# The second pass over the tokens in two pieces of 512, its operands kept by chunks of 128 tokens

## The chip, the cores and the metric

The kernel runs on one core of one Trainium2 chip. The metric is device time in microseconds (us): the median of three runs, 1899.62 us, lowest 1899.07, highest 1901.29. The profiled execution took 1902.07 us, of which 1900.3 us lie between its first and its last instruction (the span).

## The reference, cut to what matters

The program is one layer of a hybrid encoder over 2048 prompt tokens and 64 sample tokens of width 1024. A normed copy `h` of the input goes through one wide projection. Its columns feed two branches, a chunked state-space scan with a short convolution in front (SSD) and a bank of diagonal recurrences (S5). Both branches are gated and go through an output projection.

```python
h = rmsnorm(x, norm_g)
z_a, xbc, dt_raw, u_b, z_b = jnp.split(h @ w_in, IN_SPLITS, axis=-1)   # 1024 | 2048 | 16 | 1024 | 1024 columns
# SSD: xbc -> causal conv of 4 taps -> silu -> x, B, C; scan over blocks of tokens; * silu(z_a); grouped norm
# S5: u_b -> per-group diagonal recurrence -> gelu -> GLU; * silu(z_b)
out = jnp.concatenate([y_a, y_b], axis=-1) @ w_out
y = rmsnorm(x + out, final_norm_g)
```

Only `h @ w_in` is touched by the change, and of it the part for the last 1024 prompt tokens.

## The kernel before

**Two passes over the tokens.** The first pass (`st` = 0) takes the 64 sample tokens and the first 1024 prompt tokens, the second pass (`st` = 1) the other 1024. `phase_x` (L268) norms rows of 128 tokens, transposes them on TensorE into PSUM (`psx`) and splits every value into a rounded part and its rest: ScalarE writes the high part (L324), VectorE the low part (L326). The tokens of a pass are held in three pieces (L37): 320, 384 and 384 tokens in the first pass, 256, 384 and 384 in the second. Each piece has a high tile `hh` and a low tile `hl` of 8 rows of depth (`k`) by its tokens. The second pass writes into the same three pairs of tiles, so a piece of the second pass may be written once the piece of the first pass in that place has been read for the last time.

**The projection.** Weights come in blocks of 256 columns, in two halves of depth: `wblock` (L215) loads a half, ScalarE rounds it (`CAST whi`, L212) and VectorE forms the rest (`wlo`). Three halves can be held at a time, so a half is rounded only when the half three before it is no longer read. `proj_cm` (L232) takes 128 of these columns as the stationary operand and one piece of tokens as the moving one. It issues 24 matmuls for a piece (8 depths, three products each: high by high, high by low, low by high) into one of four PSUM banks. A run of 128 columns over all tokens of the second pass is thus 3 pieces, 72 matmuls. There are 32 such runs in the second pass: 16 in `phase_uz_block` (L345, the columns of the S5 input and gate, tile `psu`) and 16 in `conv_block` (L690, the columns that go through the convolution, tile `psr`). The gate of the SSD branch and dt (`proj_tm`, L242, tile `psz`) use chunks of 128 tokens as the stationary operand; there the piece only says where a chunk lies.

**What is woven between the pieces.** A piece ends in a `yield`. `weave` (L1286) runs one generator as the main line and after each of its yields advances side generators by a rate: the S5 recurrence `s5_steps` (L663) at rate 1 per yield, and the chunk scan `phase_s_chunks` (L840) at 1.8 to 2. A step of the S5 recurrence makes products on TensorE (`psi` in `s5_a`, `psy` in `s5_c`), several passes of ScalarE and VectorE, and scans on VectorE. A chunk of the SSD scan is a chain over three engines. `a1` puts transposes and one product into PSUM (`pA`) and scans decay products into `E` on VectorE; `a2` multiplies `E` by what is in `pA`; `b1` makes `pY` from `E` and from the state `h2`, and `pH`; `b2` adds `pH` to the state. So chunk c+1's product with the state waits until `b2` of chunk c is through.

**What sets the order.** The Tile scheduler takes the program in this written order and sets each engine's queue from it with its own estimates; an engine then runs its queue strictly in order, a waiting instruction holding what is behind it. Loads are issued by SyncE (SP), also in order.

Of the kernel before, what the change touches and what calls it, by code (L numbers as in the profile page):

```python
# [19 lines left out]
NS = 64  # L20
# [13 lines left out]
C_ZA, C_X, C_B, C_C, C_DT, C_U, C_ZB = 0, 1024, 2048, 2560, 3072, 3088, 4112  # L34


PIECES = ((320, 384, 384), (256, 384, 384))  # L37


ORDERED = {mybir.EngineType.Activation, mybir.EngineType.DVE}  # L40
# [3 lines left out]
def tile_hybrid_stream(  # L44
# [162 lines left out]
    hp = right.enter_context(tc.tile_pool(name="hp", bufs=1, side="right", reuse_waits="tile"))  # L207
    rawp = right.enter_context(tc.tile_pool(name="rawp", bufs=2, side="right", reuse_waits="tile"))
    wp = right.enter_context(tc.tile_pool(name="wp", bufs=3, side="right", reuse_waits="tile"))

    def split(hi, lo, raw):
        act.copy(out=hi, in_=raw)  # L212
# [18 lines left out]

    def proj_cm(ps, W, m0, piece):  # L232

        hi, lo, _ = piece
        for k in range(8):
            wh = W[0][k // 4][:, k % 4, m0:m0 + 128]
            wl = W[1][k // 4][:, k % 4, m0:m0 + 128]
            mm(ps, wh, hi[:, k], k == 0, False)
            mm(ps, wh, lo[:, k], False, False)
            mm(ps, wl, hi[:, k], False, k == 7)  # L240

    def proj_tm(ps, W, n, piece, off, nt):  # L242

        hi, lo, _ = piece
        for k in range(8):
            wh = W[0][k // 4][:, k % 4, 0:n]
            wl = W[1][k // 4][:, k % 4, 0:n]
            mm(ps, hi[:, k, off:off + nt], wh, k == 0, False)
            mm(ps, lo[:, k, off:off + nt], wh, False, False)
            mm(ps, hi[:, k, off:off + nt], wl, False, k == 7)  # L250

    def proj_smp(ps, W, n, piece):

        hi, lo, s2 = piece
        for k in range(8):
            wh = W[0][k // 4][:, k % 4, 0:n]
            wl = W[1][k // 4][:, k % 4, 0:n]

            def both():
                mm(ps[:, :n], s2[:, k], wh, k == 0, k == 7)  # L260
            if k < 7:
                both()
            mm(ps[:NS, :n], s2[:, k, 0:NS], wl, False, False)
            if k == 7:
                both()


    def phase_x(st, pcs, xpool):  # L268

        rows = [(xs, 0, NS)] if st == 0 else []  # L270
        rows += [(xp, 1024 * st + 128 * i, 128) for i in range(8)]
        g_bc = []
        live = {}

        def load(i):

            if i >= len(rows):
                return
            src, r0, n = rows[i]
            xt = xpool.tile([128, D], F32, tag="xt", name="xt", bufs=4)  # L280
            sp.dma_start(out=xt[:n], in_=src[r0:r0 + n, :])
            if not g_bc:
                g_bc.append(xpool.tile([128, D], F32, tag="g_bc", name="g_bc", bufs=1))
                sp.dma_start(out=g_bc[0], in_=norm_g[0:1, :].to_broadcast([128, D]))
            rs = cons.tile([128, 1], F32, tag="rs", name="rs", bufs=4)
            sq = xpool.tile([128, D], F32, tag="xsq", name="xsq", bufs=1)
            actf(sq[:n, :D], xt[:n], AF.Square, scale=1.0 / 32, accum_out=rs[:n])
            pool.tensor_scalar(out=rs[:n], in0=rs[:n], scalar1=1.0, scalar2=EPS, op0=ALU.mult, op1=ALU.add)
            pool.tensor_tensor(out=rs[:n], in0=rs[:n], in1=mhalf[:n], op=ALU.pow)
            live[i] = xt, rs  # L290

        def norm(i):
            if i >= len(rows):
                return
            n = rows[i][2]
            xt, rs = live[i]
            stt(xt[:n], xt[:n], rs[:n], g_bc[0][:n], ALU.mult, ALU.mult)

        load(0)
        load(1)  # L300
        norm(0)
        yield
        col = i = base = 0
        for j, (src, r0, n) in enumerate(rows):
            xn = live.pop(j)[0]
            if col == base + (PIECES[st][i] if pcs else 0):
                if pcs:
                    base += PIECES[st][i]
                    i += 1
                w = PIECES[st][i]  # L310
                hi = hp.tile([128, 8, PIECES[0][i]], F32R, tag=f"hh{i}", name=f"hh{i}")
                lo = hp.tile([128, 8, PIECES[0][i]], F32R, tag=f"hl{i}", name=f"hl{i}")
                s2 = None
                if st == 0 and i == 0:
                    s2 = hp.tile([128, 8, 2 * NS], F32R, tag="hs", name="hs")
                pcs.append((hi[:, :, :w], lo[:, :, :w], s2))
            off = col - base
            for q in range(2):
                ps = pj.tile([128, 4, 128], F32, tag="pj", name="psx")
                for k in range(4):  # L320
                    kk = 4 * q + k
                    nc.tensor.transpose(ps[:, k, :n], xn[:n, kk * 128:(kk + 1) * 128], ident[:n, :n])
                hv = pcs[i][0][:, 4 * q:4 * q + 4, off:off + n]
                act.copy(out=hv, in_=ps[:, :, :n])  # L324
                lv = pcs[i][1][:, 4 * q:4 * q + 4, off:off + n]
                tt(lv, ps[:, :, :n], hv.bitcast(F32), ALU.subtract)  # L326
                if n == NS:
                    pool.tensor_copy(out=s2[:, 4 * q:4 * q + 4, 0:NS], in_=hv.bitcast(F32))
                    pool.tensor_copy(out=s2[:, 4 * q:4 * q + 4, NS:], in_=lv.bitcast(F32))
            col += n  # L330
            norm(j + 1)
            load(j + 2)
            yield


    def kcols(st):

        if st == 0:
            return [(0, 0, 64, 0), (0, 64, 256, 9), (1, 0, 384, 41), (2, 0, 384, 89)], 137, 0
        return [(0, 0, 256, 0), (1, 0, 384, 32), (2, 0, 384, 80)], 129, 137  # L340

    def phase_uz_block(st, pcs, blk, kind):
        runs, K, c0 = kcols(st)
        W = wblock([((C_U if kind == "u" else C_ZB) + 256 * blk, 256)])
        piece_outer = st == 0 and blk == 3 and kind == "z"  # L345
        ubs, ths = {}, {}
        order = [(m, i) for i in range(3) for m in range(2)] if piece_outer else [(m, i) for m in range(2) for i in range(3)]
        for m, i in order:
            b = 2 * blk + m
            if i == 0:  # L350
                ubs[m] = big.tile([128, 8, 137], F32, tag="big", name="ub")
                pool.memset(ubs[m][:, :, 8:9] if st == 0 else ubs[m][:, :, 128:129], 0.0)
            ub = ubs[m]
            ps = pj.tile([128, 512], F32, tag="pj", name="psu")
            proj_cm(ps[:, :PIECES[st][i]], W, 128 * m, pcs[i])
            for (pi, off, n, k0) in runs:
                if pi != i:
                    continue
                nk = n // 8
                src = ps[:, off:off + n].rearrange("p (k s) -> p s k", s=8)  # L360
                dst = ub[:, :, k0:k0 + nk]
                if kind == "u":
                    act.copy(out=dst, in_=src)
                else:
                    actf(dst, src, AF.Silu)
            if i < 2:
                yield
                continue
            if kind == "u":
                for j in range(8):  # L370
                    pool.dma_start(out=U[8 * b + j, :, :, c0:c0 + K].rearrange("s c k -> c s k"),
                                   in_=ub[16 * j:16 * j + 16, :, :K])
            else:
                pool.dma_start(out=Z[:, 128 * b:128 * b + 128, c0:c0 + K].rearrange("s c k -> c s k"), in_=ub[:, :, :K])
            yield


    def prep_params(p, P):
# [311 lines left out]
    def conv_block(st, pcs, W, m0, blk, p):  # L690
# [6 lines left out]
        else:  # L697
            act.copy(out=R[:, 0:3], in_=carry[:, blk, :])
        o = 3
        for i in range(3):  # L700
            n = PIECES[st][i]
            ps = pj.tile([128, 512], F32, tag="pj", name="psr")
            proj_cm(ps[:, :n], W, m0, pcs[i])
            if st == 0 and i == 0:
# [3 lines left out]
            else:  # L708
                act.copy(out=R[:, o:o + n], in_=ps[:, :n])
                o += n  # L710
            yield
        if st == 0:
            act.copy(out=cnew[:, 0, :, blk], in_=R[:, 64:67])
            act.copy(out=carry[:, blk, :], in_=R[:, 1091:1094])
# [9 lines left out]
    def chunks(st):  # L724

        r = []
# [3 lines left out]
            for c in range(6):  # L730
                r.append((128, 1 + c // 3, 128 * (c % 3), 323 + 128 * c, 320 + 128 * c))
        else:
            r += [(128, 0, 0, 0, 1088), (128, 0, 128, 128, 1216)]
            for c in range(6):
                r.append((128, 1 + c // 3, 128 * (c % 3), 256 + 128 * c, 1344 + 128 * c))
        return r

    def phase_s_init(st, p):
# [547 lines left out]
    def weave(main, *sides):  # L1286

        acc = [0.0] * len(sides)
        for _ in main:
            for i, (g_, r_) in enumerate(sides):  # L1290
                acc[i] += r_
                while acc[i] >= 1.0:
                    acc[i] -= 1.0
                    next(g_, None)
# [5 lines left out]
    def take(g_, n):  # L1300

        for _ in range(n):
            next(g_, None)
            yield

    V = {}
    pcs = []
# [69 lines left out]
    weave(S[2], (S5, R5))  # L1377
    C = chks(2)
    weave(phase_uz_block(1, pcs, 3, "z"), (C, RB), (S5, R5))
    weave(take(S[3], 12), (C, 1), (S5, R5))  # L1380
    drain(C, S5)
    s5_out(p5, fin)
    aux.close()
# [67 lines left out]
```

## Time and profile before

| What | us |
|---|---|
| median of three runs | 1899.62 |
| profiled execution, span | 1902.07, 1900.3 |
| TensorE matmuls busy | 1831.1 (96%) |
| TensorE weight loads busy (beside the matmuls) | 1709.4 (90%) |
| VectorE, ScalarE, GpSimd busy | 1096.5 (58%), 908.6 (48%), 378.3 (20%) |
| span up to the first matmul of the second pass's pieces | 692.86 |
| from there to the last matmul of its convolutions | 572.24 |

TensorE is busy for all but 4% of the span. Its single matmuls overlap (the next one starts while the last one drains), so the duration that a row gives for one matmul is longer than the time that it costs; the cost is read from the distance between starts.

### The profile page before, as it was taken

What the parts mean: (1) busy time and instruction counts of PE and PEld (TensorE: products, weight loads), DVE (VectorE), ACT (ScalarE), POOL (GpSimd) and SP (SyncE); (2) the same over time, 40 slices, a digit from 0 to 9 for tenths busy, and PEclk for the clock granted to TensorE, in tenths of its full rate; (3) what the DMA queues carried; (4) which work ended last, traced back from release to release, by engine and by line L of the source; (5) the groups of instructions that cost most, each with busy time, mean ns of one, the idle gap of its engine ahead of it and who ended that gap; (6) DMA issues with size and microseconds to landing.
All of it is one profiled execution on the core that took longest, in us unless ns stands there. A gap on an engine that the chain in (4) does not pass through costs nothing. (4 is left out here: it accounts for less than half of the span.)

```text
span 1900.3 us, 31061 instructions
## 1 busy us (share of the span) xinstructions
PE 1831.1 (96%) x11400; PEld 1709.4 (90%) x11400; DVE 1096.5 (58%) x2157; ACT 908.6 (48%) x2505; POOL 378.3 (20%) x730
## 2 busy tenths in 40 slices
PE   7998999999899899999999999999999999999998
PEld 6998999999899799889989999998999988887886
DVE  5688687685767653776678567857544432212221
ACT  5466465545646633666666556656544421111110
POOL 3022314233332411032013301212211000001000
PEclk9999999999999999999999999999999999999999
DMA  5224545454444454456545754536455553313220
GB/s 165 76 72 101 155 105 137 127 137 103 121 128 111 143 137 119 139 153 182 152 136 164 206 159 125 152 95 178 134 161 161 186 181 92 97 56 95 92 86 34
DMA packets 197816, 244.69 MB, mean 129 GB/s; under 512 B 41696, under 2 KB 158432, under 8 KB 197664
## 3 DMA queue, kind: packets, MB, share of 16 engines
q1 hardware_dynamic: 170944, 167.49, 31.7%
q0 software_dynamic: 25136, 74.66, 13.4%
q8 instruction: 90, 1.47, 0.3%
q10 hardware_dynamic: 1584, 0.56, 0.2%
q14 instruction: 62, 0.51, 0.1%
HBM read 171.09 MB, written 75.75 MB: 130 GB/s over the span
## 5 line engine op out<-in xcount | busy, mean ns | idle before, releaser
L69 PE MATMUL psp<-whi,yy 128*128 128x512 f32 x1056 | 333.6, 394 | 1.3 <-ACT yy L212 1.3
L69 PE MATMUL psu<-hh,whi 128*128 128x384 f32 (+2 forms) x768 | 259.1, 337 | 0.8 <-DVE hl L60 0.8
L69 PE MATMUL psr<-hh,whi 128*128 128x384 f32 (+2 forms) x768 | 256.8, 335 | 3.1 <-ACT whi L212 3.1
L69 PE MATMUL psr<-hh,wlo 128*128 128x384 f32 (+2 forms) x768 | 249.4, 325 | 1.8 <-DVE wlo L60 1.8
L69 PE MATMUL psu<-hl,whi 128*128 128x384 f32 (+2 forms) x768 | 250.3, 326 | 0.0
L69 PE MATMUL psu<-hh,wlo 128*128 128x384 f32 (+2 forms) x768 | 250.1, 326 | 0.0
L69 PE MATMUL psr<-hl,whi 128*128 128x384 f32 (+2 forms) x768 | 249.9, 325 | 0.0
L69 PEld LDWEIGHTS psp<-whi,yy 128*128 128x128 f32 x1056 | 198.2, 188 | 48.9 <-ACT yy L212 1.5
L69 PE MATMUL psp<-wlo,yy 128*128 128x512 f32 (+1 forms) x544 | 214.8, 395 | 0.0
L69 PE MATMUL psz<-whi,hh 128*128 128x256 f32 (+1 forms) x512 | 151.4, 296 | 0.4 <-DVE dtr L60 0.4
L69 PEld LDWEIGHTS psr<-hh,whi 128*128 128x128 f32 x768 | 146.1, 190 | 4.5 <-ACT whi L212 3.3
L69 PE MATMUL psz<-whi,hl 128*128 128x256 f32 (+1 forms) x512 | 147.0, 287 | 1.4 <-DVE hl L60 1.4
L69 PEld LDWEIGHTS psr<-hh,wlo 128*128 128x128 f32 x768 | 145.7, 190 | 2.5 <-DVE wlo L60 2.3
L69 PEld LDWEIGHTS psu<-hh,whi 128*128 128x128 f32 x768 | 145.4, 189 | 2.1 <-DVE hl L60 1.0
L69 PEld LDWEIGHTS psr<-hl,whi 128*128 128x128 f32 x768 | 146.0, 190 | 1.2
L69 PE MATMUL psz<-wlo,hh 128*128 128x256 f32 (+1 forms) x512 | 147.0, 287 | 0.0
L69 PE MATMUL psg<-gh,glo 128*128 128x266 f32 x512 | 146.1, 288 | 0.9 <-DVE glo L60 0.9
L69 PE MATMUL psg<-gl,ghi 128*128 128x266 f32 x512 | 146.6, 289 | 0.0
L69 PEld LDWEIGHTS psu<-hl,whi 128*128 128x128 f32 x768 | 145.5, 189 | 1.1
L69 PEld LDWEIGHTS psu<-hh,wlo 128*128 128x128 f32 x768 | 145.3, 189 | 0.3
L69 PE MATMUL psg<-gh,ghi 128*128 128x266 f32 x512 | 144.0, 288 | 0.0
L60 DVE TENSOR_TENSOR wlo<-raw,whi 128x1024 fp32r<-128x1024 f32 (+1 forms) x80 | 97.9, 1225 | 78.9 <-ACT whi L212 77.3
(559 smaller groups left out, 3914.6 us busy)
## 6 DMA issues: line engine op xcount, KB each, us to landing
raw<-in_w_in_dram SPq DMA_DIRECT2D x64, 512.0 KB
tab<-TAB SPq DMA_DIRECT2D x64, 266.0 KB
xt<-in_x_prompt_dram SPq DMA_DIRECT2D x32, 512.0 KB
abc<-atd SPq DMA_DIRECT2D x64, 256.0 KB
TAB<-k POOLq DMA_DIRECT2D x32, 266.0 KB, 3.7
ut<-U SPq DMA_DIRECT2D x32, 266.0 KB
Y<-bs POOLq DMA_DIRECT2D x32, 266.0 KB, 3.8
G<-Y SPq DMA_DIRECT2D x128, 66.5 KB
```

The source lines that it names most:

```text
L60: dve.tensor_tensor(out=out, in0=a, in1=b, op=op)
L69: nc.tensor.matmul(out, lhsT=lhsT, rhs=rhs, start=start, stop=stop)
```

## The change

In the second pass there are two pieces of 512 tokens in place of 256, 384 and 384. One tile `HL` takes the place of the three pairs `hh` and `hl`. In the first pass its parts are laid out as the pairs were: each piece high then low, depth by tokens. In the second pass the same tile is laid out by chunks of 128 tokens: for each chunk, high and low, 8 depths of 128 tokens. The moving operand of a matmul of the second pass, 512 tokens of one depth, is then four runs of 128 elements that lie 2048 elements apart; the output in PSUM is one run of 512. A class `Piece` hides the two layouts. A yield of the second pass's pieces counts 1.5 in `weave`, so that the side work per run of 128 columns keeps its amount, and `take(S[3], 12)` becomes 8 because four runs now have 8 pieces.

```diff
-PIECES = ((320, 384, 384), (256, 384, 384))
+PIECES = ((320, 384, 384), (512, 512))
+PARTW = (1, 1.5)
+class Piece:
...
+    def mov(self, h, k):
+        if self.chunks is None:
+            return self.hl[h][:, k]
+        return self.chunks[:, :, h, k]
...
+    def put(self, h, q, off, n):
+
+        if self.chunks is None:
+            return self.hl[h][:, 4 * q:4 * q + 4, off:off + n]
+        return self.chunks[:, off // 128, h, 4 * q:4 * q + 4, :n]
...
+    HL = [hp.tile([128, 16 * sum(PIECES[0])], F32R, name="HL")]
+    HOFF = [16 * sum(PIECES[0][:i]) for i in range(3)]
...
-            mm(ps, wh, hi[:, k], k == 0, False)
-            mm(ps, wh, lo[:, k], False, False)
-            mm(ps, wl, hi[:, k], False, k == 7)
+            mm(ps, wh, piece.mov(0, k), k == 0, False)
+            mm(ps, wh, piece.mov(1, k), False, False)
+            mm(ps, wl, piece.mov(0, k), False, k == 7)
...
+                    pcs.append(Piece(w, chunks=HL[0][:, 8192 * i:8192 * i + 8192].rearrange("p (c h k t) -> p c h k t", c=4, h=2, k=8)))
...
-        return [(0, 0, 256, 0), (1, 0, 384, 32), (2, 0, 384, 80)], 129, 137
+        return [(0, 0, 512, 0), (1, 0, 512, 64)], 129, 137
...
-            if i < 2:
-                yield
+            if i < np_ - 1:
+                yield PARTW[st]
...
-        for _ in main:
+        for w in main:
             for i, (g_, r_) in enumerate(sides):
-                acc[i] += r_
+                acc[i] += r_ * (w or 1)
...
-    weave(take(S[3], 12), (C, 1), (S5, R5))
+    weave(take(S[3], 8), (C, 1), (S5, R5))
```

**ScalarE's queue, second pass, second weight block of the first convolutions.** Before: `bs<-b` and `bs<-psy` belong to the S5 recurrence, `cv` and `R` to the convolution, `whi` to the weights that TensorE needs next.

```order
L66 ACTIVATE cv<-cv 128x1024
L709 COPY R<-psr 128x384
L642 COPY bs<-b 64x532
L660 COPY bs<-psy 128x266
L643 ACTIVATE bs<-b 64x532
L660 COPY bs<-psy 128x266
L212 CAST whi<-raw 128x4x256
```

The same place now:

```order
L92 ACTIVATE cv<-cv 128x1024
L653 COPY b<-psi 128x265
L654 COPY bs<-psi 64x265
L655 ACTIVATE bs<-psi 64x265
L653 COPY b<-psi 128x265
L654 COPY bs<-psi 64x265
L655 ACTIVATE bs<-psi 64x265
L240 CAST whi<-raw 128x4x256
```

The rounding of the weights no longer stands behind `bs<-b`, which waits for VectorE's scans; the copies ahead of it wait only for the products `psi`.

**TensorE's queue, second pass, a chunk of the SSD scan amid the columns of the S5 input.** Before, a chunk's group of products is followed by S5 products and by matmuls of a piece:

```order
L69 MATMUL pY<-xd,E 128x64 x4
L69 MATMUL pY<-h_103,cv 128x256
L69 MATMUL pH<-xw,bt 128x256
L856 MATMUL pA<-ident,cv 128x128
L857 MATMUL pA<-ident,cv 128x128
L858 MATMUL pA<-ident,cv 128x128
L69 MATMUL pA<-cv 128x128
L69 MATMUL psy<-ut,ct 128x266
```

Now, at the fourth and fifth chunk of the first block that is woven:

```order
L95 MATMUL pY<-xd,E 128x64 x4
L95 MATMUL pY<-h_103,cv 128x256
L95 MATMUL pH<-xw,bt 128x256
L884 MATMUL pA<-ident,cv 128x128
L885 MATMUL pA<-ident,cv 128x128
L886 MATMUL pA<-ident,cv 128x128
L95 MATMUL pA<-cv 128x128
L95 MATMUL pY<-xd,E 128x64 x4
L95 MATMUL pY<-h_103,cv 128x256
L95 MATMUL pH<-xw,bt 128x256
```

Two chunks' groups stand one behind the other, with no matmul of a piece between the first chunk's `pH` and the second chunk's product with the state. This occurs three times in the second pass now and did not before.

**TensorE's queue, second pass, where that first woven block begins.** Before; `pA<-cv` (the product of the convolved B and C) stands a whole piece of 384 further on:

```order
L69 MATMUL psu<-hl_7463,whi 128x256
L856 MATMUL pA<-ident,cv 128x128
L857 MATMUL pA<-ident,cv 128x128
L858 MATMUL pA<-ident,cv 128x128
L69 MATMUL psi<-ut,bl 128x265 x2
L69 MATMUL psu<-hh_7657,whi 128x384
```

The same place now:

```order
L95 MATMUL psu<-HL,whi 128x512 x2
L884 MATMUL pA<-ident,cv 128x128
L885 MATMUL pA<-ident,cv 128x128
L886 MATMUL pA<-ident,cv 128x128
L95 MATMUL psi<-ut,bl 128x265
L95 MATMUL pA<-cv 128x128
L95 MATMUL psi<-ut,bl 128x265
L95 MATMUL psu<-HL,whi 128x512 x2
```

`pA<-cv` has moved up, from behind the second piece to behind the first.

## Rows read from the trace of the kernel before

**Rows 1.** The page: span, and TensorE's busy time (share of the span).

```profile
span 1900.3 us, 31061 instructions
PE 1831.1 (96%) x11400; PEld 1709.4 (90%) x11400; DVE 1096.5 (58%) x2157; ACT 908.6 (48%) x2505; POOL 378.3 (20%) x730
```

**Rows 2.** Windows: stretch, length, busy time (count) by engine, TensorE's granted clock, DMA.

```profile
692.86:1265.10 572.24, 557.03 (x3495) 533.28 (x3494) 394.59 (x667) 336.96 (x920) 109.14 (x223) 0.99 0.53 148
...
769.00:776.00 7.00, 5.78 (x20) 5.06 (x21) 5.68 (x7) 4.95 (x13) 0.00 (x0) 0.51 0.88 253
974.00:977.40 3.40, 3.40 (x14) 3.06 (x13) 1.44 (x3) 2.17 (x10) 0.00 (x0) 0.52 0.64 160
```

**Rows 3.** Timeline, TensorE, second pass: start, duration, line, tiles, shape.

```profile
692.86 0.28 PE L69 MATMUL psu<-hh,whi 128*128 128x256 f32 x1
...
695.70 0.34 PE L69 MATMUL psu<-hh,whi 128*128 128x384 f32 x1
...
704.09 0.28 PE L69 MATMUL psu<-hh,whi 128*128 128x256 f32 x1
...
737.77 0.27 PE L813 MATMUL pa<-ident,slots 128*128 128x128 f32 x1
```

**Rows 4.** Timeline, TensorE, output projection: the first matmul of a tile, and what follows it.

```profile
1582.90 0.48 PE L69 MATMUL psp<-wlo,yy 128*128 128x512 f32 x1
...
1605.18 0.38 PE L1146 MATMUL pso<-ident,ya 128*128 128x128 f32 x2
```

**Rows 5.** Groups of ScalarE over the whole span: count, busy us and mean ns.

```profile
L324 ACT CAST hh<-psx 128x512 fp32r<-128x512 f32 x32 | 17.4, 589 | 2.3 <-PE psx L322 1.9
L212 ACT CAST yy<-pso 128x512 fp32r<-128x512 f32 x32 | 17.2, 590 | 56.1 <-PE pso L1146 56.1
```

**Rows 6.** Timeline, TensorE, second pass, a piece that follows S5 products, and the next.

```profile
922.44 0.47 PE L69 MATMUL psr<-hh,whi 128*128 128x256 f32 x1
...
925.47 0.34 PE L69 MATMUL psr<-hh,whi 128*128 128x384 f32 x1
```

**Rows 7.** Timeline of ScalarE, then what TensorE's `psr` waited for (us, times).

```profile
763.38 0.46 ACT L709 COPY R<-psr 128x384 f32<-128x384 f32 x1
765.92 0.63 ACT L642 COPY bs<-b 64x532 f32<-64x532 f32 x1 [2.08 <-DVE b L640]
...
767.89 1.05 ACT L212 CAST whi<-raw 128x1024 fp32r<-128x1024 f32 x1
...
  ACT whi L212: 3.1, 1
  DVE wlo L60: 1.2, 1
```

**Rows 8.** Groups of TensorE in 967.3 to 977.4 and in 1161 to 1170.

```profile
L69 PE MATMUL pA<-cv 128*128 128x128 f32 x4 | 1.1, 372 | 2.2 <-ACT cv L66 2.2
...
L69 PE MATMUL pA<-cv 128*128 128x128 f32 x4 | 0.9, 300 | 1.3 <-ACT cv L66 1.3
```

**Rows 9.** Groups of the convolution, whole span: ScalarE, VectorE, ScalarE.

```profile
L66 ACT ACTIVATE cv<-R,colp 128x1024 f32<-128x1024 f32 x16 | 19.9, 1242 | 0.1
...
L57 DVE SCALAR_TENSOR_TENSOR cv<-R,colp,cv 128x1024 f32<-128x1024 f32 x48 | 61.4, 1279 | 11.3 <-ACT cv L66 10.7
...
L66 ACT ACTIVATE cv<-cv 128x1024 f32<-128x1024 f32 x16 | 17.0, 1061 | 36.8 <-DVE cv L57 36.7
```

**Rows 10.** Timeline, first pass, two chunks' groups in a row: TensorE, then VectorE.

```profile
623.98 1.00 PE L69 MATMUL pY<-xd,E 128*128 128x64 f32 x8
...
627.44 1.07 PE L69 MATMUL pY<-xd,E 128*128 128x64 f32 x8 [0.99 <-DVE E L60]
...
627.88 0.41 DVE L60 TENSOR_TENSOR h<-h,pH 128x256 f32<-128x256 f32 x1
```

**Rows 11.** Group of TensorE, 692.86 to 1265.1, S5 products with their waits.

```profile
L69 PE MATMUL psy<-ut,ct 128*128 128x266 f32 x128 | 39.7, 391 | 3.3 <-DVE h L60 1.5 <-DVE E L60 0.7 <-PE psr L69 0.6
```

More of the change, by code (lines that the diff above doesn't have):

```diff
@@ L34, with __init__, out, tok @@
 C_ZA, C_X, C_B, C_C, C_DT, C_U, C_ZB = 0, 1024, 2048, 2560, 3072, 3088, 4112
-PIECES = ((320, 384, 384), (256, 384, 384))
+PIECES = ((320, 384, 384), (512, 512))
+PARTW = (1, 1.5)
+class Piece:
+    def __init__(self, w, hi=None, lo=None, s2=None, chunks=None):
+        self.w, self.hl, self.s2, self.chunks = w, (hi, lo), s2, chunks
+    def mov(self, h, k):
+        if self.chunks is None:
+            return self.hl[h][:, k]
+        return self.chunks[:, :, h, k]
+    def out(self, ps):
+        return ps if self.chunks is None else ps.rearrange("p (c t) -> p c t", t=128)
+    def tok(self, h, k, off, n):
+        if self.chunks is None:
+            return self.hl[h][:, k, off:off + n]
+        return self.chunks[:, off // 128, h, k, :n]
+    def put(self, h, q, off, n):
+        if self.chunks is None:
+            return self.hl[h][:, 4 * q:4 * q + 4, off:off + n]
+        return self.chunks[:, off // 128, h, 4 * q:4 * q + 4, :n]
 ORDERED = {mybir.EngineType.Activation, mybir.EngineType.DVE}
@@ L232, in proj_cm @@
     def proj_cm(ps, W, m0, piece):
-        hi, lo, _ = piece
+        ps = piece.out(ps)
         for k in range(8):
@@ L237, in proj_cm @@
             wl = W[1][k // 4][:, k % 4, m0:m0 + 128]
-            mm(ps, wh, hi[:, k], k == 0, False)
-            mm(ps, wh, lo[:, k], False, False)
-            mm(ps, wl, hi[:, k], False, k == 7)
+            mm(ps, wh, piece.mov(0, k), k == 0, False)
+            mm(ps, wh, piece.mov(1, k), False, False)
+            mm(ps, wl, piece.mov(0, k), False, k == 7)
     def proj_tm(ps, W, n, piece, off, nt):
-        hi, lo, _ = piece
         for k in range(8):
@@ L247, in proj_tm @@
             wl = W[1][k // 4][:, k % 4, 0:n]
-            mm(ps, hi[:, k, off:off + nt], wh, k == 0, False)
-            mm(ps, lo[:, k, off:off + nt], wh, False, False)
-            mm(ps, hi[:, k, off:off + nt], wl, False, k == 7)
+            mm(ps, piece.tok(0, k, off, nt), wh, k == 0, False)
+            mm(ps, piece.tok(1, k, off, nt), wh, False, False)
+            mm(ps, piece.tok(0, k, off, nt), wl, False, k == 7)
     def proj_smp(ps, W, n, piece):
-        hi, lo, s2 = piece
+        s2 = piece.s2
         for k in range(8):
@@ L310, in phase_x @@
                 w = PIECES[st][i]
[L311 to L316, printed above, removed]
+                if st == 0:
+                    o, n8 = HOFF[i], 8 * w
+                    hi, lo = (HL[0][:, o + h * n8:o + h * n8 + n8].rearrange("p (k t) -> p k t", t=w) for h in range(2))
+                    s2 = hp.tile([128, 8, 2 * NS], F32R, tag="hs", name="hs") if i == 0 else None
+                    pcs.append(Piece(w, hi, lo, s2))
+                else:
+                    pcs.append(Piece(w, chunks=HL[0][:, 8192 * i:8192 * i + 8192].rearrange("p (c h k t) -> p c h k t", c=4, h=2, k=8)))
             off = col - base
@@ L322, in phase_x @@
                     nc.tensor.transpose(ps[:, k, :n], xn[:n, kk * 128:(kk + 1) * 128], ident[:n, :n])
-                hv = pcs[i][0][:, 4 * q:4 * q + 4, off:off + n]
+                hv = pcs[i].put(0, q, off, n)
                 act.copy(out=hv, in_=ps[:, :, :n])
-                lv = pcs[i][1][:, 4 * q:4 * q + 4, off:off + n]
+                lv = pcs[i].put(1, q, off, n)
                 tt(lv, ps[:, :, :n], hv.bitcast(F32), ALU.subtract)
+                s2 = pcs[i].s2
                 if n == NS:
@@ L346, in phase_uz_block @@
         ubs, ths = {}, {}
-        order = [(m, i) for i in range(3) for m in range(2)] if piece_outer else [(m, i) for m in range(2) for i in range(3)]
+        np_ = len(PIECES[st])
+        order = [(m, i) for i in range(np_) for m in range(2)] if piece_outer else [(m, i) for m in range(2) for i in range(np_)]
         for m, i in order:
@@ L374, in phase_uz_block @@
                 pool.dma_start(out=Z[:, 128 * b:128 * b + 128, c0:c0 + K].rearrange("s c k -> c s k"), in_=ub[:, :, :K])
-            yield
+            yield PARTW[st]
     def prep_params(p, P):
@@ L699, in conv_block @@
         o = 3
-        for i in range(3):
-            n = PIECES[st][i]
+        for i, n in enumerate(PIECES[st]):
             ps = pj.tile([128, 512], F32, tag="pj", name="psr")
@@ L710, in conv_block @@
                 o += n
-            yield
+            yield PARTW[st]
         if st == 0:
@@ L732, in chunks @@
         else:
-            r += [(128, 0, 0, 0, 1088), (128, 0, 128, 128, 1216)]
-            for c in range(6):
-                r.append((128, 1 + c // 3, 128 * (c % 3), 256 + 128 * c, 1344 + 128 * c))
+            for c in range(8):
+                r.append((128, c // 4, 128 * (c % 4), 128 * c, 1088 + 128 * c))
         return r
@@ L1302, in take @@
         for _ in range(n):
-            next(g_, None)
-            yield
+            yield next(g_, None)
     V = {}
```

## The prediction

> **What bounds the kernel now.** I read the page first, then a table by stretches, then TensorE's timeline at the pieces, then the groups with waits. TensorE is busy for 1831.1 of 1900.3 us [rows 1], so time can come only from work that TensorE no longer does or from its waits. The change touches the second pass: from its first piece to its last convolution TensorE is busy for 557.0 of 572.2 us at a granted clock of 0.99 [rows 2]. Matmuls overlap there, so I take costs from distances between starts. One piece of 256 takes 695.70 - 692.86 = 2.84 us (24 matmuls, 118.3 ns each), the two pieces of 384 behind it 704.09 - 695.70 = 8.39 us (48, 174.8 ns each). A run of 128 columns over all tokens takes 11.23 us, and four of them end at 737.77, 44.91 us after the first start, which is again 11.23 each [rows 3]. In the output projection, where a moving operand is 512 wide, 96 matmuls and one return from transposes take 1605.18 - 1582.90 = 22.28 us [rows 4].
>
> So TensorE is bound by columns, not by the number of matmuls: from 256 to 384 columns a matmul gets 56.5 ns longer for 128 columns, and only 118.3 - 2 x 56.5 = 5.3 ns of it do not depend on the width. Merging pieces can save that fixed part, the returns from side work, and waits that hang on where a piece ends.
>
> **The change part by part.** All sums are made against the profiled execution, 1902.07 us (span 1900.3 and 1.8 around it); the median of the runs shown is 2.45 us lower.
>
> *Fewer matmuls.* There are 32 runs of 128 columns, and each goes from 72 matmuls to 48, so 768 matmuls go and the columns stay. With the row of 512 as it stands (22.28 / 96 = 232.1 ns) a run takes 11.14 us; with the one return in that row taken out (0.19 us, below) it is 230.1 ns and 11.04 us. That saves 0.09 to 0.19 us a run, 2.8 to 5.9 us in all. I take 4.4, the middle, since both ends come from one row. The rows put the fixed part at about 5 ns a matmul. The Trainium skill's page "TensorE: Matmul & The Clock Gate" (section "Wait — 56ns, not 53.3ns?") says that a matmul at full clock costs its columns at 2.4 GHz plus about 2.5 ns. This would be 109.2 ns for 256 columns where the row has 118.3, so the trace disagrees; by the rule the saving is an estimated 768 x 2.5 ns = 1.9 us, and the forecast 2.5 us later.
>
> *Jumps in the moving operand.* The 1536 matmuls of 512 now read four runs of 128 elements, three jumps each. No moving operand in this trace has jumps. A jump can't give time back, so the lower bound is nothing. The upper one is a matmul's fixed part, as if each run were a matmul of its own: 5.3 ns x 3 x 1536 = 24.4 us. The nearest row of an engine that steps over the same kind of gap is ScalarE's rounding into `hh`, four runs of 128 that lie apart, at 589 ns, against 590 ns for the same size into one run [rows 5]. I take nothing and keep the upper end for a rival.
>
> *Fewer returns.* After S5 products a piece of 256 takes 925.47 - 922.44 = 3.03 us, against 2.84 in rows 3, so a return to the projection costs 0.19 us [rows 6]. In the written order TensorE returns to it 91 times in the second pass before and 83 times now: 1.5 us.
>
> *Three waits of TensorE that hang on the order.* At 765.6 TensorE waits 3.1 us for `whi` and 1.2 us for `wlo` of the second half of a weight block. The rounding starts at 767.89 because it stands in ScalarE's queue behind `bs<-b`, which waited 2.08 us for VectorE's scan [rows 7]. Behind this wait the granted clock is 0.51 for 7.0 us (the level of 1.2 GHz instead of 2.4) [rows 2], of which 1.2 are the second wait: (7.0 - 1.2) x 0.49 = 2.8 us. Together 7.1 us. In the new order the rounding stands ahead of `bs<-b`, behind six copies that wait only for `psi`. A half block can be rounded when the half three before it is read out, which is in the middle of the last piece of the block before, and it is needed in the middle of the next piece: that distance was half a piece of 384 and half a piece of 256, 2.1 + 1.4 = 3.5 us, and is now two halves of 512, 5.5 us. The second wait is 2.2 us at 973.3 for the convolved `cv`, and again the clock falls, to 0.52 over 3.4 us: 2.2 + 1.6 = 3.8 us. The third, 1.3 us, is of the same kind at 1169 [rows 2, 8]. In both places TensorE now has a piece of 512 and S5 products, and in the first half of a second piece, ahead of the waiting `pA<-cv`. These three are worth 12.2 us. I count three quarters, 9.1 us: a new order removes these and brings small ones of the kind that S5's products show (3.3 us over 128 of them [rows 11]), which I can't place.
>
> *A wait that it adds at the first woven block.* There `pA<-cv` moves ahead of the second piece. Its chain after the last convolution piece is a copy (0.59, the width of rows 5), 1.24, three times 1.28 and 1.06 us, together 6.7 us [rows 5, 9]. TensorE covers this with S5 products and one piece, some 7.8 us, but ScalarE first has to finish a rounding and two copies, some 2.3 us. So the wait is between nothing and 1.5 us, or 3.1 with a fall of the clock as at 973. I take 1.5. What is queued behind it on TensorE is an S5 product and the next piece; ScalarE and VectorE then get their next piece late too, but they have work.
>
> *Two chunks in a row, three times.* The first pass has this once: the second chunk's `pY` waits 0.99 us for `E`, and `h` is ready only at 628.29, 4.3 us after the first `pY` (623.98) [rows 10]. There four matmuls of a piece fill the gap ahead of the product with the state; now nothing does. With `E` late it costs 1.0 to 1.2 us, with `E` early about 0.5 us (the state alone). I take 0.8 each, 2.5 us, with 1.5 and 6 us as bounds (2 us each if VectorE's scans of S5 come between).
>
> *The rest.* The side work per run is the same (2 x 1.5 for 3 x 1). Wider copies out of PSUM are fewer on ScalarE, which is busy for 337 of 572 us there [rows 2]; four PSUM banks leave each copy more than a piece's time. The one tile for all pieces adds no wait: the chunks of the new layout become free with the same pieces of the first pass, and up to the first piece of the second pass TensorE's queue is the same. These I cost at nothing; the cover is a piece of 5.5 us, and if it were gone each late copy would cost its 0.6 us.
>
> Sum: -4.4 - 1.5 - 9.1 + 1.5 + 2.5 = -11.0 us, so 1891.1 for the profiled execution and 1888.6 for a median like the one shown: 1889.
>
> **The rivals.**
> *The waits come back.* The scheduler has moved everything after the first piece, and other waits of 2 to 3 us appear, with falls of the clock behind them. For it: every place where S5, the scan and the weights meet on ScalarE has moved. Against it: the distance that weights have has grown by 2 us at each block. Then the matmuls and returns (5.9 us) remain, less the 4.0 us added: 1902.07 - 1.9, a median of 1897.7; with some of the waits gone 1895 to 1899.
> *The jumps cost (slower).* Place: the moving reads of the 1536 matmuls. At 5.3 ns a jump it adds 24.4 us, so 1913. It decides from 11.0 us / 4608 jumps = 2.4 ns a jump. For it: TensorE has no spare time, and no row shows it free. Against it: ScalarE's rows 5. The Trainium skill's page "SBUF — State Buffer" (section "Door 1: The DMA port swizzle") says that full bandwidth needs two hits in each 16-byte line, which runs of 128 floats have all along; by it a jump costs nothing, and no run here shows that for TensorE.
> *The added waits are dear (slower).* Both kinds at their upper bounds with a fall of the clock at each, 3.1 + 3 x 3.6 = 13.9 us in place of 4.0, and half of the old waits back: 1902.07 - 5.9 - 6.1 + 13.9, a median of 1901.5.
> *All goes well.* The three waits go whole, the matmuls save 5.9, the added waits cost 1.5: 1902.07 - 18.1, a median of 1881.5.
>
> **How the numbers follow.** The forecast (1883 to 1895) gets 0.63, the waits that come back 0.18, the jumps 0.07, the dear added waits 0.05, all goes well (to 1883 and below) 0.07. The range from 1880 to 1899 leaves out the jumps, most of the dear waits and a little below. A measurement of this kernel tells about 0.2% from no change, 1895.8 to 1903.4. Faster takes the forecast, the good case and almost half of the waits that come back: 0.78. The same is the rest of these and most of the dear waits: 0.14. Slower is the jumps and a little: 0.08.
>
> **What would show it.** In the new profile a run of 128 columns without side work should take 11.04 to 11.14 us between starts, 230 to 232 ns a matmul; 235 ns or more means that jumps cost. TensorE should have no wait for `whi` or `wlo` in the second pass's first convolutions, and the granted clock should stay up there. The three places with two chunks in a row should show waits of `pY` for `E` or `h` of about 0.5 to 1.2 us, and the first `pA<-cv` of the first woven block one of up to 1.5 us. The first pass and all after the second pass should take the same time as before. The forecast is wrong if 572 us of the second pass shrink by less than 5 us or if a new wait above 2 us with a fall of the clock stands in it.

## The result, and where the time went

The changed kernel takes 1915.1 us in the median (1906.6 to 1922.2), the kernel before in the same series 1901.6 us (1899.1 to 1903.6). The ratio is 1.0066, with an interval from 1.0051 to 1.0081: it is slower, by some 12.5 us by the ratio (13.5 by the medians), where 1889 us was forecast. The profiled execution took 1914.0 us, against 1902.1 before.

The page of the changed kernel, first lines:

```profile
span 1912.3 us, 29498 instructions
...
PE 1835.1 (96%) x10632; PEld 1641.3 (86%) x10632; DVE 1096.1 (57%) x2157; ACT 903.2 (47%) x2473; POOL 381.1 (20%) x730
```

Against [rows 1] 768 matmuls are gone, and TensorE is busy for longer. The table of stretches says where (columns as in [rows 2]): first the second pass, then three stretches inside it.

```profile
693.55:1275.77 582.22, 557.62 (x2728) 462.24 (x2726) 393.81 (x667) 331.21 (x888) 111.91 (x223) 0.99 0.52 145
803.20:810.00 6.80, 5.13 (x12) 3.70 (x13) 3.37 (x5) 4.67 (x13) 0.11 (x1) 0.50 0.77 209
888.60:892.00 3.40, 3.21 (x11) 2.82 (x12) 0.35 (x1) 1.88 (x5) 0.00 (x0) 0.50 0.61 217
1011.50:1014.90 3.40, 3.25 (x8) 2.58 (x9) 2.86 (x7) 1.96 (x7) 3.38 (x7) 0.50 0.62 135
```

The second pass starts 0.7 us later than before and takes 582.2 us instead of 572.2 [rows 2], so 10.0 of the 11.9 us between the two profiled executions lie in it. Both signs that the prediction named for being wrong are there: the pass grew, and new waits above 2 us stand in it with a fall of the clock. The granted clock is at its lower level there for 13.6 us, before for 10.4 [rows 2]; the places are others. The view of waits of TensorE over the second pass (total us, times, longest) says what stands ahead of them:

```profile
PE psi L95 <- DMA ut<-U: 8.6, 3, 3.6
PE pA L95 <- ACT cv L92: 3.4, 3, 1.4
PE psy L95 <- DVE h L86: 3.2, 3, 1.7
PE psi L95 <- issue: 2.3, 1, 2.3
PE psi L95 <- DVE h L86: 1.5, 4, 0.4
PE pso L969 <- DVE h L86: 1.4, 2, 1.2
PE pY L95 <- DVE h L86: 1.2, 1, 1.2
```

Before, `psi` never waited for `ut`, and the longest waits of the pass were those of [rows 7, 8]. The three new ones are of two kinds. SyncE's queue and TensorE's timeline, changed kernel, at the first two:

```profile
768.06 0.39 SPq L250 DMA_DIRECT2D raw<-in_w_in_dram  x1
768.55 0.45 SPq L636 DMA_DIRECT2D ut<-U  x1
...
773.02 1.16 PE L95 MATMUL psi<-ut,bl 128*128 128x265 f32 x4 [2.34 <-DMA ut<-U]
...
797.67 0.38 SPq L250 DMA_DIRECT2D raw<-in_w_in_dram  x1
799.39 0.45 SPq L639 DMA_DIRECT2D tab<-TAB  x1
800.01 0.46 SPq L636 DMA_DIRECT2D ut<-U  x1
...
803.90 1.25 PE L95 MATMUL psi<-ut,bl 128*128 128x265 f32 x2 [2.68 <-DMA ut<-U]
806.12 0.80 PE L95 MATMUL pA<-cv 128*128 128x128 f32 x2 [0.96 <-ACT cv L92]
```

`ut` has two buffers, so a load may be issued once `psy` has read the tile two steps back. In the kernel before it was issued just as that reading ended in 23 of 30 steps, and 0.2 to 2.4 us later in the other seven. Here it is issued 4.4 and 5.1 us after `psy` is through, because in SyncE's queue it stands behind a load of weights (`raw`) that waits for VectorE's `wlo`, and the second time behind one of `tab` too. The third is different; TensorE's timeline, with SyncE's two loads:

```profile
881.72 0.37 SPq L250 DMA_DIRECT2D raw<-in_w_in_dram  x1
882.49 0.36 SPq L636 DMA_DIRECT2D ut<-U  x1
...
881.85 0.61 PE L95 MATMUL psy<-ut,ct 128*128 128x266 f32 x2
...
884.84 0.40 PE L95 MATMUL psz<-whi,HL 128*128 128x256 f32 x2
888.79 2.11 PE L95 MATMUL psi<-ut,bl 128*128 128x265 f32 x4 [3.55 <-DMA ut<-U]
```

`ut` is issued at once, but `psi` is due (its start less its wait) 2.8 us after `psy` has read the old tile for the last time, and the load is there only 6.3 us after its issue. In the kernel before, this distance from the end of the last reading to the start of `psi` was 6.0 us or more in every one of 30 steps. In the changed kernel it is 5.8 us or more in the other 29: of the three waits, one comes from a short distance and two from the queue. A second profiled execution of the changed kernel has the same three waits (2.2, 1.4 and 4.7 us).

What was forecast as gain came. The first two starts below span the 192 matmuls of the first four runs without side work [rows 3]:

```profile
693.55 0.62 PE L95 MATMUL psu<-HL,whi 128*128 128x512 f32 x2
...
738.03 0.27 PE L841 MATMUL pa<-ident,slots 128*128 128x128 f32 x1
...
768.09 0.50 PE L95 MATMUL psr<-HL,wlo 128*128 128x512 f32 x1 [0.27 <-DVE wlo L86]
```

They take 44.48 us instead of 44.91, or 231.7 ns a matmul, and the wait for `whi` and `wlo` of [rows 7] has shrunk from 4.3 to 0.27 us (third line).

### The profile page after: what moved, and what is told of

The parts are those of the page before. It is cut to its first block, busy times and chain, and to the rows that moved or that the text cites. A ratio compares the mean times of both kernels' runs of the same rounds, so it can differ in the third digit from the quotient of the medians.

```text
span 1912.3 us, 29498 instructions
## 1 busy us (share of the span) xinstructions
PE 1835.1 (96%) x10632; PEld 1641.3 (86%) x10632; DVE 1096.1 (57%) x2157; ACT 903.2 (47%) x2473; POOL 381.1 (20%) x730
## 5 line engine op out<-in xcount | busy, mean ns | idle before, releaser
L95 PE MATMUL psu<-HL,whi 128*128 128x512 f32 (+2 forms) x1280 | 365.1, 366 | 0.0
L95 PE MATMUL psr<-HL,whi 128*128 128x384 f32 (+2 forms) x1280 | 355.4, 360 | 0.0
L95 PEld LDWEIGHTS psu<-HL,whi 128*128 128x128 f32 x1280 | 233.4, 191 | 21.7
L95 PEld LDWEIGHTS psr<-HL,whi 128*128 128x128 f32 x1280 | 232.8, 189 | 21.9
L95 PE MATMUL psu<-HL,wlo 128*128 128x384 f32 (+2 forms) x640 | 230.4, 361 | 0.0
L95 PE MATMUL psr<-HL,wlo 128*128 128x512 f32 (+2 forms) x640 | 227.0, 355 | 0.4 <-DVE wlo L86 0.3
L95 PE MATMUL psz<-whi,HL 128*128 128x256 f32 (+1 forms) x1024 | 196.7, 292 | 1.8 <-DVE HL L86 1.4
L95 PEld LDWEIGHTS psz<-whi,HL 128*128 128x128 f32 x1024 | 163.0, 193 | 4.3 <-DVE HL L86 2.3
L95 PE MATMUL psz<-wlo,HL 128*128 128x256 f32 (+1 forms) x512 | 147.6, 289 | 0.0
L83 DVE SCALAR_TENSOR_TENSOR cv<-R,colp,cv 128x1091 f32<-128x1091 f32 (+1 forms) x96 | 126.2, 1315 | 20.2 <-ACT cv L92 17.1
```

The lines of the kernel that those rows point to most:

```text
L83: dve.scalar_tensor_tensor(out=out, in0=in0, scalar=s, in1=in1, op0=op0, op1=op1)
L95: nc.tensor.matmul(out, lhsT=lhsT, rhs=rhs, start=start, stop=stop)
```

## The experiments

Theory A: the new waits come from the order of SyncE's queue. Theory B: they come from the larger lots in which the side work is let in (a weight of 1.5 after each half of a run, where it was 1 after each of three pieces). Rival C: the layout or the width of the operands costs. All ratios are to the kernel before, on the same chip, from 4 to 10 executions of each kernel. "Pass" is the time from the start of the first `psu` to that of the last `psr` of the second pass in the profiled execution: 572.0 us before, 581.8 in the changed kernel. It is one execution each, and the same kernel's passes differ by some us (581.8 and 583.5; quarters 566.0 and 569.5), so only larger differences of it count.

| kernel | ratio, interval | pass, us |
|---|---|---|
| changed | 1.0066 (1.0051 to 1.0081) | 581.8 |
| changed, again | 1.0066 (1.0046 to 1.0086) | 583.5 |
| layout alone | 1.0002 (0.9992 to 1.0012) | 572.4 |
| pieces of 512, old places of the side work | 0.9977 (0.9968 to 0.9987) | 567.5 |
| old pieces, larger lots | 1.0119 (1.0104 to 1.0134) | 593.4 |
| S5 at the old places, chunks in lots | 1.0000 (0.9989 to 1.0012) | 578.1 |
| chunks at the old places, S5 in lots | 1.0048 (1.0031 to 1.0064) | 578.6 |
| third buffer for weights | 1.0054 (1.0039 to 1.0069) | 584.6 |
| `ut` on GpSimd's queue | 1.0079 (1.0058 to 1.0100) | 583.9 |
| weights on GpSimd's queue | 1.0113 (1.0092 to 1.0134) | 584.9 |
| third buffer for `ut` | 1.0014 (1.0002 to 1.0026) | 575.6 |
| the same, chunks put off | 0.9992 (0.9979 to 1.0006) | 571.0 |
| quarters | 0.9976 (0.9961 to 0.9991) | 566.0 |
| quarters, chunks put off | 0.9981 (0.9968 to 0.9994) | 567.9 |
| eighths | 0.9957 (0.9939 to 0.9974) | 563.7 |
| eighths, chunks put off | 0.9953 (0.9937 to 0.9970) | 562.9 |
| old pieces, sixths | 1.0015 (1.0002 to 1.0027) | 574.9 |

**Layout alone.** The pieces and the written order of before, in the new tile.

```diff
-PIECES = ((320, 384, 384), (512, 512))
+PIECES = ((320, 384, 384), (256, 384, 384))
-PARTW = (1, 1.5)
+PARTW = (1, 1)
```

> The kernel before, with its pieces of 256, 384 and 384 and its written order, but the pieces laid out by chunks of 128 tokens in one tile, so that moving operands are read in two or three runs of 128. Theories A and B: the same as before, 1900 to 1903. Rival C (the layout costs): slower, 1908 to 1915.

1.0002: rival C falls. Reading a moving operand in runs of 128 values costs nothing that can be measured, and neither does one tile for all pieces.

**The old places of the side work, with pieces of 512.** `proj_cm` yields inside a piece, at a quarter and at five eighths of a run, and not at the end of the first piece.

```diff
+            if k == cut:
+                yield 1
...
+            yield from proj_cm(ps[:, :n], W, m0, pcs[i], (4, 2)[i] if st else None)
```

> The changed kernel with its pieces of 512 and its layout, but the side work is let in where the kernel before let it in: after a quarter, five eighths and the whole of each run of 128 columns (inside a piece), with weight 1 each. SyncE's order is then the one of before but for some weight loads late in the pass. Theories A and B: the new waits of psi go and the three old waits (12.2 us with the clock's falls) come back; what is left of the change are the matmuls, 3.4 us: 1897 to 1900. Rival C: 1911 to 1915, since layout and width are unchanged.

0.9977, some 4.3 us faster than before: on balance the 3.4 us of the matmuls, and little else. Layout and width are those of the changed kernel, so its 0.9% are the weave's. Here `psi` waits for `ut` nowhere, and the waits for weights of [rows 7] are back in part:

```profile
PE psr L95 <- ACT whi L240: 1.7, 1, 1.7
PE psr L95 <- DVE wlo L86: 0.8, 1, 0.8
```

**Larger lots with the old pieces.**

```diff
             if i < 2:
-                yield
+                if st == 0 or i:
+                    yield (1, 1.5)[st]
```

> The kernel before, its pieces of 256, 384 and 384 and its layout, but the side work of the second pass is let in only after five eighths and after the whole of each run, with weight 1.5 each, as the change lets it in after a half and the whole. Theory B (larger lots of side work make the waits): the waits of the changed kernel appear here too, and the matmuls saved do not: 1.006 to 1.011 of before. Rival D (the waits come from pieces of 512, for instance from their wider copies out of PSUM, and not from the lots): 0.999 to 1.002 of before.

1.0119, even above what B gave. Its waits of TensorE are of the same kinds:

```profile
PE pA L69 <- ACT cv L66: 5.8, 3, 2.5
PE psi L69 <- DMA ut<-U: 4.0, 1, 4.0
PE psy L69 <- issue: 3.2, 2, 2.0
PE psy L69 <- DVE h L60: 2.4, 2, 2.0
```

So B holds, with neither the layout nor the width there. (The two lots are not evenly spaced here, at five eighths and at the end of a run; what this adds is not shown.)

**Which side work.** The weave weighs a yield by the generator it feeds: for one kind the places and weights of the run above, for the other those of the change.

```diff
-                acc[i] += r_ * (w or 1)
+                t_ = THIRDS if g_ is V.get("S5") else LOTS
+                acc[i] += r_ * (t_[w] if w in t_ else w or 1)
```

> The changed kernel, but only S5's steps are let in at a quarter, five eighths and the whole of each run with weight 1; the chunks stay in lots of 1.5 pieces' worth after each piece. If S5's lots make the waits (ut loaded too late for psi): 0.997 to 1.000 of before. If the chunks' lots do (two groups in a row, banks of PSUM not yet free, late h): 1.004 to 1.007. If each makes a part, in between.

> The mirror of that: the chunks are let in at a quarter, five eighths and the whole of each run with weight 1, S5's steps stay in lots of 1.5 after each piece. If S5's lots make the waits: 1.004 to 1.007 of before. If the chunks' lots do: 0.997 to 1.000.

1.0000 and 1.0048. Set against 0.9977 with both at the old places, the chunks' lots cost 0.0023 (4.4 us) and S5's lots 0.0071 (13.5 us); the sum, 0.0094, is about the 0.0089 between both in lots and neither. By the ratios the larger part is S5's. The passes do not show this split: 578.1 and 578.6 us, each some 11 above 567.5. The profiled execution with S5 at its old places was the slowest of its ten (1910.6 us, median 1907.0), and `psi` still waits for `ut` once in it (3.2 us). So the size of the split rests on the medians.

**What of S5's lots.** Three edits were made on the changed kernel against the waits for `ut`. In the first, every third half block of weights goes into a buffer of its own:

```diff
+            if NRAW and n <= 256 and NRAW[0] % 3 == 0:
+                raw = hp.tile([128, 4, 256], F32, tag="hs", name="raw")
```

> The changed kernel with a third buffer for half a weight block in the second pass, so a weight load waits for the wlo of three halves back instead of two. The written order of TensorE, ScalarE and VectorE is the changed kernel's, row for row. Theory A (SyncE's queue: a weight load that waits for wlo now stands ahead of S5's load of ut, so psi gets ut late): the waits of psi for ut (8.6 us: 2.34 at 773.0, 2.68 at 803.9, 3.55 at 888.8) go, and with them the falls of the granted clock at 803 and 889, about 12 us in all: 1902 to 1905. Rival B (the side work comes in larger lots, so that ut is asked for too shortly before its use, whatever stands ahead of it): the psi waits stay, 1912 to 1915. Rival C (the moving operand in runs of 128 or the one tile for all pieces): 1915.

1.0054, and `psi` waits 10.8 us for `ut`. As it was expected this would speak for B, but the edit did not take the waiting load away: ahead of the first two late `ut` stand the 67th and the 69th weight load in place of the 66th and the 68th, released by the same `wlo` (the 50th and the 52nd). So it tells nothing on A. In the second and the third, `ut` or the weights leave SyncE's queue (`pool.dma_start` for `sp.dma_start`):

> The changed kernel with S5's load of ut issued on GpSimd's DMA queue instead of SyncE's; the other S5 loads and the weight loads stay where they are. Theory A: ut no longer stands behind a waiting weight load, the psi waits for ut go, 1902 to 1906; GpSimd now waits for psy before each ut, which could delay its stores and rs by a few us without TensorE noticing. Rival B: ut is still issued only when psy has read the old one and then takes its 3 to 4 us to land, so psi still waits, 1911 to 1915. Rival C: 1915.

> The changed kernel with the weight loads of the second pass on GpSimd's DMA queue, so that none can stand ahead of S5's loads in SyncE's. If the queue's order made the two waits of psi at 773 and 804 (ut issued 4.4 and 5.1 us after psy had left it): both go, ut is issued at once, and the third at 889 (2.4 us between psy and psi) stays; 5 to 7 us less than the changed kernel if nothing stands behind them, 2 to 4 us if the wait for cv takes the place of that at 804: 1.002 to 1.006 of before. If the queue's order has no part: as the changed kernel.

Neither gains (1.0079 and 1.0113). With the weights gone, the wait at the first place is gone and `ut` is issued at once. At the second place SyncE's queue shows what then holds it:

```profile
796.98 1.09 SPq L641 DMA_DIRECT2D tab<-TAB  x2
798.21 0.49 SPq L639 DMA_DIRECT2D bl<-MATS  x1
811.37 0.44 SPq L641 DMA_DIRECT2D tab<-TAB  x1
811.92 0.53 SPq L638 DMA_DIRECT2D ut<-U  x1
```

`tab` waits there for VectorE, `ut` is issued 6.8 us after `psy`, and `psi` waits 4.4 us. The third wait stays, as expected (3.9 us). So A in its narrow form, a weight load ahead of `ut`, is not enough; what stands ahead changes, and any load that waits will do. In this run 8 us were lost ahead of the second pass as well (its first `psu` at 706.9 against 698.7), where the two passes meet and the edit also changed the order; that part was not followed up. With `ut` on GpSimd's queue, the first two waits went but for 0.3 us, but `pA` waited 5.0 us for `cv` at 804, and `psi` 6.6 at 886.

The fourth edit gives `ut` a third buffer and issues it a step earlier, so that neither the distance nor the queue decides (`fill` loads each `ut` up to the one named, once its columns of `U` are written). VectorE's order is unchanged, TensorE's and ScalarE's nearly so.

```diff
+        if q % 3 == 2:
+            ut = hp.tile([128, 2, 512], F32, tag="hs", name="ut")[:, :, :KT]
...
+            fill(i + 1)
             nxt = s5_load(qs[i + 1], p, uts[qs[i + 1]]) if i + 1 < len(qs) else None
+            fill(i + 2)
```

> The changed kernel with a third buffer for ut (in 4 KB that lie free in the second pass), and each ut loaded one S5 step earlier, so that neither psy's last reading nor a weight load ahead of it decides when it lands. The written order of VectorE is the changed kernel's row for row, that of TensorE and ScalarE but for 2 and 7 rows of the comparison. If psi's waits for ut are what S5's lots cost: the three waits at 773, 804 and 889 (8.6 us, with the clock's falls 12 us) go: 1.000 to 1.002 of before. If they only stand ahead of other waits (the wait of pA for cv at 804 comes in place of one, as when ut went through GpSimd's queue): one or two of them are given back, 1.003 to 1.005. If ut has no part in it: 1.006.

1.0014 against 1.0066: about 10 us by the ratios, 6 to 8 by the pass. The waits for `ut` are gone, though one has turned into another; TensorE's waits:

```profile
PE pA L95 <- ACT cv L92: 7.7, 4, 5.0
PE psy L95 <- DVE h L86: 3.3, 3, 1.7
PE psi L95 <- issue: 2.3, 1, 2.3
PE psu L95 <- DVE wlo L86: 1.7, 1, 1.7
```

The 5.0 us are `pA<-cv` at the first woven block, which stood behind `psi`'s wait in the changed kernel with 0.96 us. To take it away, the chunks' first steps there are put off by two pieces:

```diff
-    weave(uz(1), (C, RA), (S5, R5))
+    weave(uz(1), (C, RA), (S5, R5), late=2.7)
```

> The kernel with the third buffer for ut, and the first steps of the chunks in the first woven block put off by two pieces of 512 (2.7 in the weave's account). If the wait of pA for cv at 804 (5.0 us) is a price of its own that only needs distance: it goes, 5 to 7 us less than with the third buffer alone, 0.997 to 0.999 of before. If the delay only moves the wait, or the rest of the chunks then comes too late: 1.000 to 1.003.

0.9992: another 4.6 us in the pass, 0.0022 in the ratio (the intervals overlap by a little). With both edits the changed kernel is back at the time of before.

**A finer weave.** The opposite of larger lots: a yield after each half of a piece, or every two depths, with the weight cut in proportion.

```diff
+            if cut and k and k % 2 == 0:
+                yield 0.375
```

> The changed kernel with the side work let in after each quarter of a run (half a piece) with weight 0.75, so finer than before. Theory B: no lot is larger than one step of each kind, the new waits stay away, and the old three need not come back since the order is another: 0.994 to 0.999 of before; some 32 more returns to the projection cost 0.19 us each, 6 us at most. If finer is not better, 1.000 to 1.004.

> Side work after each eighth of a run (6 matmuls of 512) with weight 0.375: an even finer weave. If only the size of a lot counts, which was one step at a quarter already, nothing more is won: 0.997 to 0.999 of before. If evener spacing counts too: 0.993 to 0.997. If the returns count (0.19 us each, up to some 60 more than in quarters where a step of each kind falls apart): 1.000 to 1.003.

0.9976 and 0.9957: eighths have the lowest ratio, some 8 us under the kernel before, though the two intervals overlap. One more execution of quarters, on another chip, took 1902.3 us beside a median of 1906.6 before (0.998). Putting off the chunks was tried on both:

> Side work after each quarter of a run, and the first step of the chunks of a woven block is put off by one or two quarters (1.3 in the weave's account). If the wait of pA for cv at 804 (4.1 us, with the clock's fall about 6) only needs that distance, it goes: 0.994 to 0.997 of before. If the wait moves on to the next operation of the chunks: 0.997 to 0.999.

> Side work after each eighth of a run, and the first steps of the chunks in the first woven block put off by five eighths (3.4 in the weave's account). If the one large wait left there (pA for cv, 6.2 us) goes: 0.992 to 0.994 of before. If it moves along with the delay, as it did with quarters: 0.995 to 0.997.

Neither gains by more than its interval (0.9981 and 0.9953). With quarters the wait moved along with the chunks (4.2 us still); with eighths it fell from 6.2 to 1.3 us, and a wait of `pY` for `h` of 2.4 us took part of its place. The best version, eighths with the chunks put off, beats both kernels: 0.9953, with an interval from 0.9937 to 0.9970.

Last, the finer weave on the kernel before, with its own pieces, each cut in two:

> The kernel before, its pieces and its layout, with the side work of the second pass let in after each half of a piece (six places in a run) with weight 0.5. If the size of a lot alone decides the waits, it gains what the finer weave gains without the wide pieces: 0.996 to 0.999 of before. If the gain of quarters and eighths needed the 512-wide pieces or their longer distances for the weights: 1.000 to 1.003.

1.0015, no gain. The waits for `psr`'s weights stay there:

```profile
PE psr L69 <- ACT whi L212: 3.9, 1, 3.9
PE psr L69 <- DVE wlo L60: 1.5, 1, 1.5
```

With quarters and pieces of 512 the same stretch has 0.5 us for `wlo` and none for `whi`. So lots are not all: with the old pieces a finer weave did not pay. The waits for weights are the clearest difference between the two traces; that they alone make it is not shown.

## Why the prediction was wrong

**The failed step is "the rest", costed at nothing.** Its reason was that the side work per run is the same and that copies have time. The side work is the same in amount and not in spacing: with two places in a run instead of three, two steps of S5 or of a chunk fall into one. The loads of S5 (SyncE's queue, which that step did not look at) then come too late for `psi` (8.6 us), and products wait for `h`. `psy` reads no `h`; what it waits 3.2 us for is VectorE's update of `h`, which reads `pH` in one of the four PSUM banks that S5 and the chunks share. The 2.3 us of `psi<-issue` are likely a wait for a bank too, which is not shown. The second pass takes 581.8 us where it takes 567.5 with the side work at its old places: 14.3 us. Of these, TensorE's idle time makes 7.5 us (24.6 against 17.1), and the time at the lower clock, 13.6 against 3.4 us at half speed, up to 5; the rest is not placed. Most of S5's share is the waits for `ut` and what they pull along: by the ratios the third buffer alone wins back about 10 of the 13.5 us, by the pass 6 to 8.

**The other terms, in their order.**
- *Fewer matmuls*: 0.107 us a run, 3.4 us in all, against 4.4 forecast, within its bounds. Per matmul that went it is 4.5 ns.
- *Jumps*: nothing, as taken; the layout alone measures 1.0002. The Trainium skill's page "SBUF — State Buffer" (section "Door 1: The DMA port swizzle") asks for two hits in each 16-byte line, which runs of 128 values have; the measurement agrees.
- *Fewer returns*: 84 in the trace before and 77 now, 7 fewer where 8 were forecast; at 0.2 us each an estimated 1.4 us. No run isolates this term.
- *Three old waits*: right in size. The 7.1 us at the weights went but for 0.27; the wait of `pA` at 973 fell from 2.2 to 1.0 us without a fall of the clock; the one at 1169 stayed (1.3 to 1.4). That is some 9.6 us (6.8 + 2.8) against 9.1. Both reasons given for the weights have a part. With wide pieces and the old places `psr` still waits 1.7 and 0.8 us, with old pieces in sixths 3.9 and 1.5, so the longer distance alone does not take the wait away. Where only S5 is at the old places, 1.3 us of `whi` are left; where only S5 is in lots, none. This fits the other reason, S5's new place in ScalarE's queue; each figure is from one execution.
- *The added wait of `pA<-cv`* was mis-sized: 1.5 us, with 3.1 as its upper bound. Once `psi`'s wait no longer hides it, it is 5.0 us, and 6.2 with eighths. The chain itself was about right (0.57, 1.26, three times 1.31 and 1.06 us, against 6.7 in all). What was too short is the wait ahead of it: the last convolution piece ends at 793.5 on TensorE, and ScalarE copies it out only at 798.92 (5.4 us later, where 2.3 were forecast), behind a copy of S5 that waited for VectorE's scan and a rounding; from the changed kernel's timeline of ScalarE:

```profile
796.64 0.64 ACT L672 COPY bs<-b 64x532 f32<-64x532 f32 x1 [2.02 <-DVE b L670]
...
797.97 1.05 ACT L240 CAST whi<-raw 128x1024 fp32r<-128x1024 f32 x1
798.92 0.57 ACT L738 COPY R<-psr 128x512 f32<-128x512 f32 x1
...
799.76 1.26 ACT L92 ACTIVATE cv<-R,colp 128x1024 f32<-128x1024 f32 x1
...
805.01 1.06 ACT L92 ACTIVATE cv<-cv 128x1024 f32<-128x1024 f32 x1 [3.54 <-DVE cv L83]
```

- *Two chunks in a row*: about 0.2, 0.2 and 1.35 us, 1.75 against 2.5.

The rival "the waits come back" told this mechanism, other waits of 2 to 3 us with falls of the clock behind them, and had 0.18. Its price was wrong: it took the old 12.2 us as the most that can come back, and nothing bounds new waits by the old ones.

## What to carry to other kernels

Whoever makes the main line's steps larger also makes the lots of everything that is woven into them larger. Check, for each side chain, the distance from the last reading of a buffer to the first use of its next filling (here 6.0 us or more before, 2.8 in the worst step after, for a load that took 4 to 6), and each in-order DMA queue for a waiting load ahead of an urgent one. Cut the weave apart from the tiles: the wide pieces were worth 0.2% with the old spacing, and together with a finer weave 0.4%. A new order that removes the waits that can be seen is not to be costed at nothing elsewhere; as much may come in new places.

## What the runs showed of the hardware

- A moving operand of 512 columns read as four runs of 128 values, 8 KB apart in each partition, takes 231.7 ns between starts. A contiguous one takes 231.5 (mean of 1551 distances in the output projection of the kernel before), so no cost of the jumps can be seen.
- SyncE's queue is in order: behind a load that waits for its buffer, a load of `ut` whose buffer was free was issued 4.4, 5.1 and 6.8 us late.
- A load of 266 KB took from issue to use 4.5, 3.9 and 6.3 us in the three places of the changed kernel. A half block of weights (512 KB) was issued 0.5, 2.3 and 0.8 us ahead of it, and the DMA engines were busy for 85% of the time or more in all three, so neither tells why the third took longer. With the weights on GpSimd's queue the third still took 6.9 us.
- Around the end of waits of TensorE of 2.3 to 3.6 us the granted clock fell to 0.50 (the level of 1.2 GHz) for 3.4 or 6.8 us in three of four cases; at the wait of 2.34 us at 773 it did not (1.00 from 764 to 777). In the second profiled execution of the changed kernel the wait in the same place, 2.20 us, was followed by 3.4 us at 0.50. So the length of one wait does not tell whether the clock falls.
